# Tokens handed over transposed, norm scales applied behind the input projection, first keys taken as tokens land

## The chip, the cores and the metric

One core of a Trainium2 chip. The metric is the device time of one execution in microseconds (us). The engines are named as in the profile: PE (TensorE: matmuls and transposes; PEld its weight loads), DVE (VectorE), ACT (ScalarE), POOL (GpSimd), SP (SyncE, which issues nearly all DMAs of this kernel, in order).

## The reference

One block of a streaming encoder over 2048 tokens of 1024 channels, all in float32:

```python
h = rms_norm(x, norm_mix_g)                 # x * rsqrt(mean(x^2) + eps) * g
z = h @ w_in                                # 1024 -> 2568 columns
u_a, v_a = gelu(z[:512]), gelu(z[512:1024]) # gating heads
q, k, v  = z[1024:1536], z[1536:2048], z[2048:2560]
f        = z[2560:2568] + f_bias            # forget logits, one for each of 8 heads
out_a = u_a * (w_s @ layer_norm(v_a) + b_s) # in blocks of 128 tokens, w_s masked
out_b = softmax(q k^T / 8 + c[t] - c[s]) v  # s <= t, c = cumsum(log sigmoid(f))
x = x + concat(out_a, out_b) @ w_out
x = x + conv_ffn(rms_norm(x, norm_ffn_g))   # up, causal conv of width 3, gate, down
return rms_norm(x, norm_final_g)
```

## The kernel before

Matmuls run in single-pass float32 (`F32R`). To keep precision, both operands are split into a high and a low part, and `mm3` issues three matmuls for each 128 of the contraction: high x high, high x low, low x high. The split of a weight unit (128 x 1024 values, 512 KB) is `load_unit`: a DMA into `raw`, a cast to `whi` on POOL (`cast`), a difference `wlo` on DVE. There are two `raw` and five `whi`/`wlo` buffers.

Tokens are worked on in two halves of 1024, each of two chunks `b` of 512 (`TB`). Phase A (`phase_a`, `a_half`) computes the input projection. Half 0 goes: keys and queries, values, gating heads. Half 1 goes: gating heads, values, keys and queries. From the gating heads of half 0 on, the attention (`b_stream`) is interleaved with the projection: `tick` counts matmuls and takes a step of attention at a fixed rate; `defer` puts a piece of work a number of matmuls later. All later stages (output projection, feed-forward) follow with PE as the engine of most work.

The projection needs the tokens with channels on partitions, `hT[b]`, in high and low parts (`thi`, `tlo`). Before, `a_rows` loads rows of 128 tokens (tile `x`, four buffers), squares and sums them on ACT (L358), takes the power -1/2 on POOL (L362) and scales the rows on DVE (L366). `a_norm` transposes them on PE, four 128 x 128 transposes for each of eight channel groups of a chunk (L182), and splits the result out of PSUM with the norm's gain (ACT L191, DVE L192). For half 1 the rows are read twice: once for the scales alone and once, in column pieces that POOL scales (L399), for the transposes, which are deferred among the gating matmuls. The columns of gains, convolution weights and biases (`columns`, `columns_turn`) and the gating weights (`a_gate_w`) are transposed on PE too.

`channels` computes one key or query block: 128 channels x 512 tokens, 24 matmuls into a PSUM bank of tag `mm` (two buffers). ACT copies the high part out (L416), DVE takes the low part (L417), and four DMAs write both to DRAM (`kx`, `qx`) out of tile `vn` (four buffers). `a_forget` computes the forget logits of a chunk (16 matmuls against `wf`), and `cumulate` their running sum (matmuls against the triangle `tri`). PSUM has eight banks: two `mm`, two `tp`, three `s`, one `o`; the last four belong to attention.

The order on each engine's queue is set by the program order, `issue_after`, priorities, and the scheduler of the tile framework, which reorders instructions by a simulation of its own. An engine works its queue in order.

Of the kernel before, what the change touches and what calls it, by code (L numbers as in the profile page):

```python
# [32 lines left out]
AHEAD_B, AHEAD_W = 100, 2000  # L33
LAG = 2
# [17 lines left out]
def f32(ap):  # L52
    return ap.bitcast(F32)
# [26 lines left out]
class Block:  # L80
# [134 lines left out]
    def constants(self):  # L215
# [6 lines left out]
        self.colA = cp.tile([P, 112], F32, name="colA")  # L222
        self.colB = cp.tile([P, 88], F32, name="colB")
# [15 lines left out]
    def columns(self):  # L239

        nc, a = self.nc, self.a
        r0 = self.til(self.sp, [P, TB], F32, "st")[:112, :P]
        r1 = self.til(self.sp, [P, TB], F32, "st")[:88, :P]
        cv = a["w_conv"][0].rearrange("w (c p) -> w c p", p=P)
        self.dma(r0[0:8, :], a["norm_mix_g"][0].rearrange("(c p) -> c p", p=P))
        self.dma(r0[8:16, :], a["norm_ffn_g"][0].rearrange("(c p) -> c p", p=P))
        self.dma(r0[16:24, :], a["sg_b"][0])
        self.dma(r0[24:68, :], cv[0])
        self.dma(r0[68:112, :], cv[1])
        self.dma(r1[0:44, :], cv[2])  # L250
        self.dma(r1[44:88, :], a["b_conv"][0].rearrange("(c p) -> c p", p=P))
        self.rows_c = r0, r1
        self.g_mix = self.colA[:, 0:8]
        self.g_ffn = self.colA[:, 8:16]
        self.sgb = self.colA[:, 16:24]
        self.cw0 = self.colA[:, 24:68]
        self.cw1 = self.colA[:, 68:112]
        self.cw2 = self.colB[:, 0:44]
        self.cb = self.colB[:, 44:88]

    def columns_turn(self):
        nc = self.nc
        r0, r1 = self.rows_c
        for r, n, col in ((r0, 112, self.colA), (r1, 88, self.colB)):
            ps = self.til(self.ap, [P, TB], F32, "tp")
            nc.tensor.transpose(ps[:, :n], r, self.ident[:n, :n])
            nc.vector.tensor_copy(col, ps[:, :n])

        for t in (self.colA[:, 46:68], self.colA[:, 90:112], self.colB[:, 22:44], self.colB[:, 66:88]):
            nc.vector.tensor_scalar(t, t, 0.5, None, ALU.mult)  # L270


    def phase_a(self):
        tc = self.tc
        with ExitStack() as es:
# [4 lines left out]
            rows = self.a_rows(0, 0, True)  # L280
            self.columns()
            self.a_forget_w()
            self.a_norm(0, 0, rows, None, 0)
            self.first = []
            for c in range(2):
                with tc.issue_after(self.lo_ins[2 + 3 * c]):
                    self.first.append(self.a_unit("k", c))
            self.a_norm(0, 1, self.a_rows(0, 1, True), 16, 6)
            after = self.pow_ins

            def consts():
                with tc.issue_after(after):
                    self.a_consts(sp, pp)
                    self.b_consts()

            self.defer(16 + 6 * KC, consts)
# [9 lines left out]
    def a_forget_w(self):  # L306
        nc, a, kp = self.nc, self.a, self.sp
        wfr = kp.tile([P, 8, 8], F32, name="wfr")
        self.dma(wfr, self.w_in[:, :, 2560:2568])
        self.wf = kp.tile([P, 8, 16], F32R, name="wf")  # L310
        with self.tc.issue_after(self.rows_ins):
            nc.vector.tensor_copy(self.wf[:, :, 0:8], wfr)
            nc.vector.tensor_tensor(self.wf[:, :, 8:16], wfr, f32(self.wf[:, :, 0:8]), op=ALU.subtract)
        self.fb = kp.tile([P, 8], F32, name="fb")
        self.dma(self.fb, a["f_bias"].broadcast_to([P, 8]))
# [16 lines left out]
    def a_gate_w(self, sp, pp):  # L332

        nc, a = self.nc, self.a
        sw = self.til(sp, [P, 8, P], F32, "x")
        self.dma(sw, a["sg_w"][0].rearrange("h t s -> t h s"))
        nc.gpsimd.memset(sw[0:64, :, 64:128], 0.0)
        self.sw = sp.tile([P, 8, P], F32, name="sw")

        def turn(q):  # L340
            ps = self.transpose4(pp, "tp", [sw[:, 4 * q + i, :] for i in range(4)])
            nc.scalar.activation(self.sw[:, 4 * q:4 * q + 4, :].rearrange("p a b -> p (a b)"), ps, AF.Copy)

        self.defer(3, lambda: turn(0))
        self.defer(9, lambda: turn(1))

    def a_rows(self, half, b, keep):
# [5 lines left out]
        xs = []  # L353
        for i in range(4):
            x = self.til(sp, [P, D], F32, "x")
            self.dma(x, self.a["x"][0, t0 + i * P:t0 + (i + 1) * P, :])
            junk = self.til(sp, [P, D], BF16, "ln")
            nc.scalar.activation(junk, x, AF.Square, accum_out=ss[:, i:i + 1])  # L358
            xs.append(x)
        for q in [slice(i, i + 1) for i in range(4)] if keep else [slice(0, 4)]:  # L360
            nc.vector.tensor_scalar(rs[:, q], ss[:, q], 1.0 / D, EPS, ALU.mult, ALU.add)
            self.pow_ins = nc.gpsimd.tensor_tensor(rs[:, q], rs[:, q], self.mhalf[:, q], op=ALU.pow).ins  # L362
        if not keep:
            return rs
# [1114 lines left out]
```

## Time and profile before

| what | us |
|---|---|
| median of 3 runs (2466.55 to 2471.33) | 2469.13 |
| profiled execution, its own time | 2466.4 |
| span of the profiled execution | 2464.6 |
| PE busy in the span | 2420.7 |
| first projection matmul on PE starts | 13.87 |
| last query block of half 0 leaves PE at about | 125.6 |

Times inside an execution are counted from the start of the span. A row of the timeline gives start, duration, engine, line, operation, output<-inputs, and in brackets how long the engine was idle before it and what ended that. A row of the waits gives the total in us, the times, the longest.

### The profile page before, as it was taken

What the parts mean: (1) busy time and instruction counts of PE and PEld (TensorE: products, weight loads), DVE (VectorE), ACT (ScalarE), POOL (GpSimd) and SP (SyncE); (2) the same over time, 40 slices, a digit from 0 to 9 for tenths busy, and PEclk for the clock granted to TensorE, in tenths of its full rate; (3) what the DMA queues carried; (4) which work ended last, traced back from release to release, by engine and by line L of the source; (5) the groups of instructions that cost most, each with busy time, mean ns of one, the idle gap of its engine ahead of it and who ended that gap; (6) DMA issues with size and microseconds to landing.
All of it is one profiled execution on the core that took longest, in us unless ns stands there. A gap on an engine that the chain in (4) does not pass through costs nothing.

```text
span 2464.6 us, 32929 instructions
## 1 busy us (share of the span) xinstructions
PE 2420.7 (98%) x11082; PEld 1989.8 (81%) x11082; DVE 1740.5 (71%) x3060; ACT 1341.4 (54%) x2629; POOL 332.0 (13%) x335
## 2 busy tenths in 40 slices
PE   7999999999999999999999999999999999999998
PEld 5788878878878778788888878878888887888887
DVE  6237677565556777878878775488888887957775
ACT  4226676554355555767677673365555555444443
POOL 3214222010113311112111011100000000001000
PEclk9999999999999999999999999999999999999999
DMA  7863544767856544555555445412222329538633
GB/s 209 243 163 105 175 119 135 187 185 208 274 178 205 182 148 157 170 161 181 163 163 181 154 153 205 158 54 93 77 77 88 92 70 319 166 100 289 210 115 121
DMA packets 346244, 396.33 MB, mean 161 GB/s; under 512 B 52924, under 2 KB 222084, under 8 KB 344652
## 3 DMA queue, kind: packets, MB, share of 16 engines
q1 hardware_dynamic: 341036, 370.11, 48.8%
q0 software_dynamic: 5040, 24.12, 2.5%
q8 instruction: 88, 1.44, 0.3%
q14 instruction: 80, 0.66, 0.1%
HBM read 300.56 MB, written 93.72 MB: 160 GB/s over the span
## 4 chain that ended last, share of the span: by engine, by line
PE 88%; DMA 4%; DVE 3%; ACT 2%; issue 1%; POOL 1%; SPq 0%; POOLq 0%; DVEq 0%; ACTq 0%
PE D L1335 16%; PE mm L211 13%; PE mm L209 13%; PE mm L207 13%; PE A L1132 3%; PE A L1134 3%; PE A L1133 3%; PE o L774 2%; PE o L773 2%; PE s L786 2%; PE s L785 2%; PE s L725 2%; PE s L724 2%; PE B L1133 2%; PE B L1134 2%; PE B L1132 2%
## 5 line engine op out<-in xcount | busy, mean ns | idle before, releaser
L207 PE MATMUL mm<-thi,whi 128*128 128x512 f32 x960 | 377.4, 393 | 2.6 <-DVE vn L417 2.0
L209 PE MATMUL mm<-tlo,whi 128*128 128x512 f32 x960 | 377.5, 393 | 0.0
L211 PE MATMUL mm<-thi,wlo 128*128 128x512 f32 x960 | 376.4, 392 | 0.1
L207 PE MATMUL mm<-whi,thi 128*128 128x512 f32 x640 | 253.2, 396 | 1.1 <-DMA thi<-mixh 1.0
L211 PE MATMUL mm<-whi,tlo 128*128 128x512 f32 x640 | 251.1, 394 | 0.8 <-DMA tlo<-mixl 0.8
L209 PE MATMUL mm<-wlo,thi 128*128 128x512 f32 x640 | 250.8, 392 | 0.2 <-DVE wlo L161 0.2
L149 POOL TENSOR_SCALAR whi<-raw 128x1024 fp32r<-128x1024 f32 x108 | 126.5, 1172 | 908.4 <-PE mm L209 551.6
L733 ACT ACTIVATE s<-s,part 128x512 f32<-128x512 f32 (+3 forms) x257 | 150.8, 587 | 151.2 <-DVE part L728 85.4
L207 PEld LDWEIGHTS mm<-thi,whi 128*128 128x128 f32 x960 | 180.4, 188 | 41.8 <-DVE vn L417 2.3
L211 PEld LDWEIGHTS mm<-thi,wlo 128*128 128x128 f32 x960 | 180.5, 188 | 37.9 <-DVE wlo L161 0.6
L209 PEld LDWEIGHTS mm<-tlo,whi 128*128 128x128 f32 x960 | 180.5, 188 | 37.3
L797 DVE TENSOR_TENSOR pl<-e,ph 128x512 fp32r<-128x512 f32 (+2 forms) x212 | 136.7, 652 | 64.1 <-ACT ph L796 31.8
L161 DVE TENSOR_TENSOR wlo<-raw,whi 128x1024 fp32r<-128x1024 f32 x108 | 143.7, 1331 | 50.0 <-POOL whi L149 44.3
L791 ACT ACTIVATE e<-s 128x512 f32<-128x512 f32 (+2 forms) x227 | 116.1, 529 | 83.3 <-DVE s L789 41.6
L1335 PE MATMUL D<-wl,xh 128*128 128x512 f32 x368 | 141.5, 389 | 0.0
L1335 PE MATMUL D<-wh,xh 128*128 128x512 f32 x368 | 140.8, 389 | 0.2 <-DVE xo L1413 0.2
L207 PEld LDWEIGHTS mm<-whi,thi 128*128 128x128 f32 x640 | 120.6, 188 | 24.9 <-DMA thi<-mixh 1.4
L211 PEld LDWEIGHTS mm<-whi,tlo 128*128 128x128 f32 x640 | 120.3, 188 | 24.9 <-DMA tlo<-mixl 1.3
L209 PEld LDWEIGHTS mm<-wlo,thi 128*128 128x128 f32 x640 | 120.6, 188 | 23.2 <-DVE wlo L161 0.4
L1335 PE MATMUL D<-wh,xl 128*128 128x512 f32 x368 | 137.3, 389 | 0.0
L796 ACT ACTIVATE ph<-e 128x512 fp32r<-128x512 f32 (+2 forms) x212 | 117.2, 563 | 36.4 <-PE o L773 29.1
L728 DVE TENSOR_REDUCE part<-s 128x1 f32<-128x512 f32 x144 | 94.8, 683 | 28.3 <-PE s L725 27.6
(1885 smaller groups left out, 5786.3 us busy)
## 6 DMA issues: line engine op xcount, KB each, us to landing
raw<-in_w_up_dram SPq DMA_DIRECT2D x72, 512.0 KB
m<-kx SPq DMA_DIRECT2D x133, 256.0 KB
m<-kx SPq DMA_DIRECT2D x160, 136.0 KB
x<-act SPq DMA_DIRECT2D x84, 256.0 KB
raw<-in_w_in_dram SPq DMA_DIRECT2D x40, 512.0 KB
v<-vd SPq DMA_DIRECT2D x66, 256.0 KB
x<-in_x_dram SPq DMA_DIRECT2D x24, 512.0 KB
raw<-in_w_out_dram SPq DMA_DIRECT2D x24, 512.0 KB
```

The costliest lines, as they stand in the source:

```text
L149: self.cast_ins = self.nc.gpsimd.tensor_scalar(out, in_, 1.0, 0.0, ALU.mult, ALU.add).ins
L161: nc.vector.tensor_tensor(lo, raw, f32(hi), op=ALU.subtract)
L207: mm(ps, lhsT=ah[k], rhs=bh[k], start=k == 0, stop=False)
L209: mm(ps, lhsT=ah[k], rhs=bl[k], start=False, stop=False)
L211: self.last_mm = mm(ps, lhsT=al[k], rhs=bh[k], start=False, stop=k == n - 1).ins
L733: nc.scalar.activation(ps[:, :n], ps[:, :n], AF.Exp, scale=-1.0, bias=dst, accum_out=ls[:, tt, sb:sb + 1])
L796: nc.scalar.activation(ph[:, c], e[:, c], AF.Copy)
L797: nc.vector.tensor_tensor(pl[:, c], e[:, c], f32(ph[:, c]), op=ALU.subtract)
L1132: mm(ps, lhsT=xh[:, ks], rhs=yh[:, k, :], start=fresh and k == 0, stop=False, **kw)
L1133: mm(ps, lhsT=xh[:, ks], rhs=yl[:, k, :], start=False, stop=False, **kw)
L1134: mm(ps, lhsT=xl[:, ks], rhs=yh[:, k, :], start=False, stop=k == 3, **kw)
L1335: nc.tensor.matmul(bank[t], lhsT=x[i][:, ts], rhs=w[k], start=fresh and j == 0 and i + k == 0, stop=last and i == 1, **kw)
```

## The change

The host hands over four arrays laid out differently: the tokens transposed (`xT`, 1024 x 2048), the gating weights transposed (`sgT`), the forget columns of `w_in` as one row for each partition (`wf`), and all gains, convolution weights and biases as columns (`cols`). The transposes of these on PE go.

The scale 1/rms of a token commutes with the projection. So `hT` now holds the tokens times the gain alone (`a_split`, from SBUF, no transpose), and the scale is applied to what the projection gives. Where tokens lie on partitions (values, gating heads) it is the scale operand of the copy; forget logits take one more small DVE operation. Where tokens lie along the free dimension (keys, queries), `a_scales` spreads the scales over 128 partitions: an ACT copy of the four scale columns to 128 x 512, four transposes on PE, an ACT copy to `rb`. `channels` then has one more DVE operation: product with `rb` into a tile `st`, and the split into high and low from there.

The scales still need the rows: `a_rows` now loads them for the scales alone, in half 0 too (2 x 2 MB in addition there).

`a_start` replaces the beginning. It issues 24 transposes of the identity into an unused bank, then loads chunk 0 in eight tiles of 128 channels, with the first two key units in quarters between them, then two more key units (into `vn` buffers), the forget columns, chunk 1, and only then the rows for the scales. `first_keys` runs the first two key units of chunk 0 channel group by channel group, then units 3 and 4, the forget product, and the first two units of chunk 1: six blocks that stay in the six banks `mm`, `s` and `o` until the scales are there. Then come `a_scales` and the evacuations.

```diff
+WARM = 24
...
+    def a_start(self):
...
+            raw = v(raws[u])[:, ks, :]
+            self.dma(raw, self.w_in[:, ks, c0:c0 + P])
+            hi, lo = [t[:, ks, :] for t in parts[u]]
+            self.cast(hi, raw)
+            nc.vector.tensor_tensor(lo, raw, f32(hi), op=ALU.subtract)
...
+        for i in range(WARM):
+            nc.tensor.transpose(junk[:, i % 4 * P:(i % 4 + 1) * P], self.ident, self.ident)
+        self.hT[0] = self.parts(0)
+        xs = [self.til(sp, [P, 2, TB], F32, "x") for _ in range(4)]
+        for k in range(KC):
+            if k % 2 == 0:
+                unit(0, slice(k, k + 2))
+            self.dma(xs[k // 2][:, k % 2, :], self.a["xT"][k * P:(k + 1) * P, 0:TB])
+            self.a_split(0, k, xs[k // 2][:, k % 2, :])
+            if k % 2 == 0:
+                unit(1, slice(k, k + 2))
+        for u in (2, 3):
+            unit(u, slice(0, KC))
...
+        self.a_tokens(0, 1, None, 0)
+        self.scales[0] = [self.a_rows(0, b) for b in range(2)]
...
+    def a_scales(self, half, b):
...
+        w = self.til(sp, [P, 4, P], F32, "st")
+        nc.scalar.activation(w, self.scales[half][b].unsqueeze(2).broadcast_to([P, 4, P]), AF.Copy)
+        ps = self.transpose4(self.ap, "tp", [w[:, i, :] for i in range(4)])
+        nc.scalar.activation(self.rb[:, b, :], ps, AF.Copy)
+
+    def a_split(self, b, k, x):
+
+        hi, lo = self.hT[b]
+        self.nc.scalar.activation(hi[:, k, :], x, AF.Copy, scale=self.g_mix[:, k:k + 1])
+        self.nc.vector.scalar_tensor_tensor(lo[:, k, :], x, self.g_mix[:, k:k + 1], f32(hi[:, k, :]),
+                                            op0=ALU.mult, op1=ALU.subtract)
...
-            nc.scalar.activation(hi, ps, AF.Copy, scale=sc)
-            nc.vector.scalar_tensor_tensor(lo, ps, sc, f32(hi), op0=ALU.mult, op1=ALU.subtract)
+            t = self.til(sp, [P, TB], F32, "st")
+            nc.vector.scalar_tensor_tensor(t, ps, -0.125 if kind == "q" else 1.0, self.rb[:, b, :], op0=ALU.mult, op1=ALU.mult)
+            self.split_sb(t, hi, lo)
...
+        def first_keys():
+
+            banks = [self.til(pp, [P, TB], F32, "mm") for _ in range(2)] + [self.scores([P, TB]) for _ in range(3)]
+            banks.append(self.til(self.bpp, [P, TB], F32, "o"))
...
+            for k in range(KC):
+                for u in (0, 1):
+                    mms(u, 0, k)
+            for u, b in ((2, 0), (3, 0)):
+                for k in range(KC):
+                    mms(u, b, k)
+            self.a_forget(half, 0)
+            for u in range(2):
+                for k in range(KC):
+                    mms(u, 1, k)
+                self.a_scales(0, u)
+                for c in (range(2), range(2, 4))[u]:
+                    channels("k", c, None, None, 0, banks[c])
+            for u in range(2):
+                channels("k", u, None, None, 1, banks[u + 4])
+            for u in (2, 3):
+                channels("k", u, *self.first[u], 1)
+            self.a_forget(half, 1)
```

In the two listings of each place below, a row is line, operation, output<-inputs with the names of the program and a tile's number, shape, and how often. On PE's queue the program began with transposes of token rows, from tile `x`:

```order
L182 MATMUL mm_236<-ident,x_188 128x128
L182 MATMUL mm_241<-ident,x_188 128x128
L182 MATMUL s_246<-ident,x_188 128x128
L182 MATMUL s_251<-ident,x_188 128x128
L182 MATMUL s_256<-ident,x_188 128x128
L182 MATMUL o_261<-ident,x_188 128x128
```

Now it begins with the transposes of the identity and goes on with the first two units (`whi_190`, `whi_192`) in turn:

```order
L289 MATMUL tp_198<-ident 128x128 x24
L425 MATMUL mm_405<-thi_223,whi_190 128x512
L425 MATMUL mm_406<-thi_223,whi_192 128x512
L426 MATMUL mm_405<-tlo_225,whi_190 128x512
L427 MATMUL mm_405<-thi_223,wlo_191 128x512
L426 MATMUL mm_406<-tlo_225,whi_192 128x512
```

The transposes of tokens are gone there; key matmuls stand first. Further down on PE's queue, at the end of the first key block of before (`mm_374`), the transposes of chunk 1 (`x_316`, `x_320`) stood ahead of the second block:

```order
L211 MATMUL mm_374<-thi_233,wlo_304 128x512
L182 MATMUL tp_365<-ident,x_316 128x128
L182 MATMUL tp_381<-ident,x_316 128x128
L182 MATMUL tp_365<-ident,x_320 128x128
L182 MATMUL tp_381<-ident,x_320 128x128
L207 MATMUL mm_463<-thi_232,whi_309 128x512
```

Now, at the end of the sixth block (`o_410`), the small transposes of the forget logits and both sets of scale transposes (`st_581`, `st_631`) stand ahead of the seventh:

```order
L427 MATMUL o_410<-thi_293,wlo_193 128x512
L598 MATMUL tp_538<-ident,ln_524 128x16 x4
L183 MATMUL tp_583<-ident,st_581 128x128 x4
L183 MATMUL tp_633<-ident,st_631 128x128 x4
L208 MATMUL mm_675<-thi_292,whi_194 128x512
```

PE thus meets the scales after 160 matmuls and meets both at once. On SP's queue, the two key units followed the rows and constants of chunk 0, and the rows of chunk 1 came next:

```order
L99 DMA raw_302<-in_w_in_dram 128x8x128
L99 DMA raw_308<-in_w_in_dram 128x8x128
L99 DMA lng<-in_sg_ln_g_dram 128x512
L99 DMA x_316<-in_x_dram 128x1024
L99 DMA x_320<-in_x_dram 128x1024
```

Now, behind chunk 0 and four key units, chunk 1 (`in_xT_dram`) and three query units (`raw_784`, `raw_790`, `raw_984`) stand ahead of or among the rows for the scales:

```order
L100 DMA raw_784<-in_w_in_dram 128x8x128
L100 DMA x_314<-in_xT_dram 128x2x512
L100 DMA raw_790<-in_w_in_dram 128x8x128
L100 DMA x_322<-in_x_dram 128x1024
L100 DMA x_326<-in_x_dram 128x1024
L100 DMA x_330<-in_x_dram 128x1024
L100 DMA raw_984<-in_w_in_dram 128x8x128
L100 DMA x_334<-in_x_dram 128x1024
L100 DMA x_342<-in_x_dram 128x1024
L100 DMA x_346<-in_x_dram 128x1024
L100 DMA x_350<-in_x_dram 128x1024
L100 DMA x_354<-in_x_dram 128x1024
```

The row tiles moved behind all of the first half's tokens and seven weight units.

226 lines of the change are left out of this document (98 added, 128 removed).

## The prediction

> **What bounds the kernel now.** I read the page first, then the start by windows of 25 us, the waits of PE (TensorE), and the timeline up to 130 us.
>
> ```profile
> span 2464.6 us, 32929 instructions
> PE 2420.7 (98%) x11082; PEld 1989.8 (81%) x11082; DVE 1740.5 (71%) x3060; ACT 1341.4 (54%) x2629; POOL 332.0 (13%) x335
> ```
>
> PE is busy for 98% of the span, so a microsecond counts only if PE stops waiting for it or stops spending it. The windows (us, then busy time and count of PE, PEld, DVE, ACT, POOL, granted clock, DMA share, GB/s) show where PE is not full:
>
> ```profile
> 0.00:25.00 25.00, 15.59 (x75) 10.69 (x76) 13.27 (x32) 16.07 (x27) 7.96 (x18) 1.00 0.84 266
> 25.00:50.00 25.00, 21.58 (x114) 15.25 (x115) 17.93 (x31) 8.54 (x15) 13.28 (x22) 1.00 0.50 135
> 75.00:100.00 25.00, 23.04 (x104) 18.59 (x103) 6.95 (x10) 8.40 (x16) 11.65 (x17) 1.00 0.89 289
> ```
>
> Of the 43.9 us that PE idles in the whole span, 12.8 lie in the first 50. The waits of PE up to 120 us name them:
>
> ```profile
> PE mm L182 <- DVE rstd L361: 7.5, 1, 7.5
> PE tp L182 <- DVE tlo L192: 2.3, 2, 1.5
> PE mm L207 <- DVE vn L417: 2.0, 1, 2.0
> ```
>
> First PE waits for the first row scale, then for the splits of the second chunk, and once for a bank that a key block has not left. The timeline gives the milestones:
>
> ```profile
> 1.19 0.29 POOL masks.py:199 TENSOR_SCALAR_AFFINE_SELECT ident<-ident 128x128 f32<-128x128 f32 x1
> 4.61 1.06 ACT L358 ACTIVATE ln<-x 128x1024 bf16<-128x1024 f32 x1 [2.54 <-DMA x<-in_x_dram]
> 13.87 0.40 PE L566 MATMUL mm<-thi,wf 128*16 128x512 f32 x1 [0.80 <-DVE tlo L192]
> 48.49 0.41 PE L603 MATMUL tp<-tri,fr 128*8 128x512 f32 x1
> 49.65 0.44 PE L207 MATMUL mm<-thi,whi 128*128 128x512 f32 x1
> ...
> 49.94 0.39 PE L209 MATMUL mm<-tlo,whi 128*128 128x512 f32 x1
> ...
> 59.04 0.39 PE L211 MATMUL mm<-thi,wlo 128*128 128x512 f32 x1
> ...
> 125.66 0.60 ACT L416 ACTIVATE vn<-mm 128x512 fp32r<-128x512 f32 x1 [4.99 <-PE mm L211]
> ```
>
> No matmul of the projection starts before 13.87. From 49.94 to 59.04 lie 40 matmuls at one after another: 9.10 / 40 = 0.2275 us each. The key and query blocks of half 0 hold 16 x 24 = 384 such matmuls, the two forget products 32: 416 x 0.2275 = 94.6 us. The last block leaves PE at about 125.6 (the evacuation that waited for PE starts at 125.66). So 31 us of these 125.6 are not projection. By 49.65 PE has done three blocks and both forget products (104 matmuls, 23.7 us): 26 of the 31 lie ahead of that point.
>
> **The change, part by part.** *Transposes of tokens.* Price of four in a stream of matmuls:
>
> ```profile
> 42.72 0.60 PE L182 MATMUL tp<-ident,x 128*128 128x128 f32 x4
> 43.08 0.48 PE L568 MATMUL mm<-tlo,wf 128*16 128x512 f32 x1
> 43.40 0.39 PE L209 MATMUL mm<-tlo,whi 128*128 128x512 f32 x1
> ```
>
> From 42.72 to 43.40 stand four transposes and one matmul: 0.68 - 0.23 = 0.45 us for four. In half 1 the 16 groups of four go (7.2 us, all in a stretch where PE is nearly full), and two groups for the scales come (0.9): -6.3. Those of half 0 are counted in the milestones below, as are the 8 of the gating weights.
>
> *The start.* The 24 transposes of the identity can begin once it stands (1.19 + 0.29). Their price is that of the first and of the later transposes of before:
>
> ```profile
> 7.97 0.85 PE L182 MATMUL s<-ident,x 128*128 128x128 f32 x3
> 8.62 0.42 PE L182 MATMUL o<-ident,x 128*128 128x128 f32 x1
> ...
> 10.84 0.49 PE L182 MATMUL s<-ident,x 128*128 128x128 f32 x3
> ...
> 11.17 0.27 PE L182 MATMUL o<-ident,x 128*128 128x128 f32 x1
> ```
>
> Three take 0.65 us (0.22 each) at 8 us, and 0.33 (0.11 each) some 3 us after the first one. So 24 take about 13 x 0.22 + 11 x 0.11 = 4.1 us: until about 5.7. What the first matmul needs lands at about the same time. DMA paces:
>
> ```profile
> 7.43 1.06 ACT L358 ACTIVATE ln<-x 128x1024 bf16<-128x1024 f32 x1 [0.42 <-DMA x<-in_x_dram]
> 8.86 1.06 ACT L358 ACTIVATE ln<-x 128x1024 bf16<-128x1024 f32 x1 [0.27 <-DMA x<-in_x_dram]
> 14.71 1.04 POOL L149 TENSOR_SCALAR whi<-raw 128x1024 fp32r<-128x1024 f32 x1 [3.62 <-DMA raw<-in_w_in_dram]
> 16.45 1.47 POOL L149 TENSOR_SCALAR whi<-raw 128x1024 fp32r<-128x1024 f32 x1 [0.71 <-DMA raw<-in_w_in_dram]
> ```
>
> Consecutive tiles of 512 KB land 1.43 us apart for tokens and 1.74 for weight units; the first tile was there at 4.61, so about 3.2 us pass before the first data. Columns, the first quarter of a unit and the first token tile are about 0.5 MB: 3.2 + 1.4 = 4.6, and the first split on ACT 0.6: 5.3. I take the first matmul at 5.8. Chunk 0 with two units is 2 x 1.74 + 4 x 1.43 = 9.2 us of DMA, landed at 12.4, while PE needs 48 x 0.2275 = 10.9 us from 5.8: PE is the slower of the two. Units 3 and 4 land at 14.2 and 15.9; cast and difference take 1.17 and 1.22 (rows below), so they are ready when PE gets there at 16.7. Chunk 1 is not needed before 5.8 + (96 + 16) x 0.2275 = 31.3. PE runs 160 matmuls through, to 5.8 + 36.4 = 42.2.
>
> ```profile
> L358 ACT ACTIVATE ln<-x 128x1024 bf16<-128x1024 f32 x16 | 16.9, 1055 | 15.2 <-DMA x<-in_x_dram 14.9
> L161 DVE TENSOR_TENSOR wlo<-raw,whi 128x1024 fp32r<-128x1024 f32 x13 | 15.8, 1218 | 3.8 <-POOL whi L149 3.7
> L149 POOL TENSOR_SCALAR whi<-raw 128x1024 fp32r<-128x1024 f32 x13 | 15.2, 1169 | 31.6 <-PE mm L209 21.7 <-DMA raw<-in_w_in_dram 5.2 <-issue 4.6
> L417 DVE SCALAR_TENSOR_TENSOR vn<-mm,vn 128x512 fp32r<-128x512 f32 x16 | 11.0, 689 | 32.8 <-ACT vn L416 26.7 <-DMA qx<-vn 4.9 <-DMA kx<-vn 1.2
> L362 POOL TENSOR_TENSOR rstd<-rstd,mhalf 128x1 f32<-128x1 f32 (+1 forms) x10 | 7.2, 721 | 35.0 <-DVE rstd L361 35.0
> ```
>
> *The new wait.* All six banks are then full, and PE's next work stands behind the transposes of both scales; the second needs all eight row tiles of half 0, 4 MiB that before did not read separately. Ahead of and with them SP issues 7 weight units (12.2 us), 8 tiles' worth of transposed tokens and 8 of rows (16 x 1.43 = 22.9), columns and layer-norm gains (1.0): 36.1 us, last landing at 39.3. Square 1.06, a small DVE step, power 0.72: about 41.3. That beats PE's 42.2 by a hair. The chain behind (two sets of transposes with ACT copies of 0.6 between, DVE 0.69 to free the first bank) still costs PE 2 to 3 us, nothing covers it, and the third unit's block of chunk 1 starts at about 45.0. The power waits in POOL's queue behind the cast of a query unit, which waits for the first unit's last use (about 36.7 + 1.2): early enough.
>
> *The rest of half 0.* 256 matmuls (58.2), two cumulations at 49.65 - 48.49 = 1.16, small transposes 0.4: 45.0 + 60.9 = 105.9. SP must write six blocks at once:
>
> ```profile
> 77.78 2.37 SPq L99 DMA_DIRECT2D kx<-vn  x4
> ```
>
> 2.4 us each, 14 us, and the constants besides. A bank is now free after one DVE operation that needs no ACT, so PE has some 11 us of cover; if the write buffers hold DVE longer, the query blocks are late next. I allow one wait like the 2.0 at L417: 107.9, against 125.6 before: -17.7.
>
> *Added evacuation.* 32 x 0.69 = 22 us of DVE. Half 0 has room (6.95 of 25 above). In half 1 it is 11 us beside this:
>
> ```profile
> 525.00:550.00 25.00, 25.00 (x119) 20.04 (x118) 15.90 (x42) 15.97 (x33) 2.11 (x2) 1.00 0.47 123
> ```
>
> PE is full while DVE works 64%; about 2 us more in each 25 stays under 75%. Nought to 4 us; I take 0. Scaled copies of values and gates keep their count. POOL loses 32 scalings that PE does not wait for: 0.
>
> **Sum**: -17.7 - 6.3 = -24.0. The profiled execution took 2466.4 (span 2464.6 and 1.8 around it), so 2442.4; it stands 2.7 under the median of 2469.13, so a median of 2445.1.
>
> **Rivals.**
>
> *Scales come later.* Over windows of 10 us the DMA rate varied:
>
> ```profile
> 10.00:20.00 10.00, 8.53 (x47) 5.79 (x46) 8.40 (x19) 5.85 (x11) 3.06 (x3) 1.00 0.95 284
> 20.00:30.00 10.00, 9.40 (x44) 6.58 (x43) 7.41 (x13) 4.57 (x9) 7.37 (x13) 1.00 0.68 194
> ```
>
> The queue up to the last row tile is 12.4 MB. At 284 GB/s throughout it lands at 46.9, and by the same steps the blocks resume at about 51: 6 later, 2451. For it: token tiles wait for four buffers. Against: 1.43 us per 512 KB is 367 GB/s. Chance 0.16.
>
> *Slower: the same wait, long.* At the second window's 194 GB/s the last tile lands at 67 and PE resumes at 71.5, 26 later: 2471. Break-even is at 200 GB/s; at 175 it is 2478. For it: one SP queue issues everything in order, and a unit waiting for its buffer stops the row tiles behind it. Against: the 194 was an emptied queue (DMA share 0.68), and the units ahead of the last row tile wait for buffers that are freed before 30 us. Chance 0.03.
>
> *Given back later.* Attention is interleaved with half 1, and the order of both changes far past this stage. PE there waits for others already:
>
> ```profile
> 225.00:250.00 25.00, 23.11 (x122) 19.56 (x122) 23.28 (x38) 14.87 (x25) 15.54 (x9) 1.00 0.56 164
> PE s L724 <- DMA m<-kx: 2.5, 1, 2.5
> PE o L774 <- DVE pl L797: 2.1, 2, 1.7
> PE s L758 <- DVE m L742: 1.9, 1, 1.9
> ```
>
> About 31 us of idle lie behind 50 us; if they grew by three quarters, the gain would be gone: 2468. For it: DVE at 93% there. Against: the change adds nothing to DVE there. Chance 0.06. If the three waits shown, all before 400 us (6.5 us), vanish instead, since PE's transposes and their banks are gone: 2439, chance 0.10.
>
> *No warm start.* Should transposes not raise the clock, the first 3 us of matmuls would go at half pace, 1.5 us later: 2447, chance 0.05. The rows speak against it: pace doubled during transposes alone. The Trainium skill, "TensorE: Matmul & The Clock Gate", Part 4, says that the full clock "doesn't engage" for transposes, as they don't count as PE activity; the trace disagrees (0.22 to 0.11 us).
>
> **Numbers.** The forecast, 2445, has the remaining 0.60. The range of 2433 to 2457 takes in the late scales (2451) with 4 us of DVE wait and the measurement on one side, and the vanished waits with no new stall at the scales (2439 - 6) on the other. A measurement of this kernel tells 0.2% (4.9 us) from no change. Faster: 0.60 + 0.16 + 0.10 + 0.05 = 0.91; the same: 0.06; slower: 0.03.
>
> **What would show it.** Right: the first projection matmul near 6 us; no PE wait over 1 us until about 42, then 2 to 3 us for the second scale's transposes; the last query block's evacuation near 108; PE's instruction count 98 lower; DVE busy time some 20 us higher. Wrong: matmuls of the first two units waiting on token tiles beyond 17 us, the resumption behind 50, or more PE waits between 225 and 400 us than the 6.5 shown.

## The result and the profile after

The changed kernel takes 2444.85 us (median of 2441.62 to 2448.11), the kernel before on the same chip 2467.84 (2464.51 to 2471.33): a ratio of 0.9907, interval 0.9887 to 0.9927. The forecast was 2445.0. The total came out; one of its two terms did not.

The page of the changed kernel, profiled in an execution of 2441.62 us:

```profile
span 2439.9 us, 32802 instructions
PE 2410.8 (99%) x10984; PEld 1982.3 (81%) x10984; DVE 1750.5 (72%) x3086; ACT 1350.3 (55%) x2635; POOL 315.9 (13%) x303
```

PE's busy time falls by 9.9 us and its idle time by 14.8 (43.9 to 29.1). The first two windows of 25 us (columns as in the prediction) are where most of the idle time went:

```profile
0.00:25.00 25.00, 21.96 (x100) 18.19 (x101) 16.48 (x30) 10.97 (x15) 7.22 (x18) 1.00 0.94 279
25.00:50.00 25.00, 23.68 (x110) 17.76 (x109) 9.20 (x19) 16.10 (x29) 9.89 (x16) 1.00 0.93 327
```

PE works 45.64 of these 50 us, against 37.17 before, and the DMA share stands at 0.94 and 0.93 where it was 0.84 and 0.50. PE's waits of more than 1 us from its first matmul or transpose up to 120 us (total, times, longest):

```profile
PE tp L183 <- ACT st L358: 1.3, 1, 1.3
PE mm L425 <- ACT thi L365: 1.3, 1, 1.3
```

The 7.5 us for the first row scale is gone, and nothing waits for token tiles. Two waits are left that matter: one for the first split (L365) and one for the second scale's copy (L358). The timeline shows both, and the last query block of half 0:

```profile
1.54 4.38 PE L289 MATMUL tp<-ident 128*128 128x128 f32 x24 [1.54 <-POOL ident masks.py:199]
5.04 1.28 ACT L365 ACT_TABLE_LOAD   x1 [5.04 <-DMA x<-in_xT_dram]
6.33 2.20 ACT L365 ACTIVATE thi<-x,cols 128x512 fp32r<-128x512 f32 x3
7.20 0.70 PE L425 MATMUL mm<-thi,whi 128*128 128x512 f32 x2 [1.27 <-ACT thi L365]
...
41.68 1.06 ACT L347 ACTIVATE ln<-x 128x1024 bf16<-128x1024 f32 x1
43.11 1.02 POOL L349 TENSOR_TENSOR rstd<-rstd,mhalf 128x4 f32<-128x4 f32 x1 [2.93 <-DVE rstd L348]
44.83 0.66 PE L183 MATMUL tp<-ident,st 128*128 128x128 f32 x4
45.52 0.60 ACT L360 ACTIVATE u<-tp 128x512 f32<-128x512 f32 x1 [1.55 <-PE tp L183]
46.13 0.62 ACT L358 ACTIVATE st<-rstd 128x512 f32<-128x512 f32 x1
46.80 0.66 PE L183 MATMUL tp<-ident,st 128*128 128x128 f32 x4 [1.32 <-ACT st L358]
47.22 0.48 PE L208 MATMUL mm<-thi,whi 128*128 128x512 f32 x1
...
109.70 0.69 DVE L398 SCALAR_TENSOR_TENSOR st<-mm,u 128x512 f32<-128x512 f32 x1 [1.42 <-PE mm L212]
```

The first tile is there at 5.04, but ACT then loads its function table for 1.28 us before it splits it: the first matmul starts at 7.20. (In the kernel before this load ran from 0.79, ahead of the first data.) The last query block's evacuation begins at 109.70, against 125.66 before: 16.0 us earlier.

Where the rest of the 24.7 us of span went is read from four marks: that evacuation, the first tanh of the feed-forward (ACT, 771.8 before and 753.7 after), the first matmul of the second half's up projection (1612.4 and 1585.5), and the end. Windows cut near these marks, of the kernel before and then of the changed one, columns as above:

```profile
126.00:772.00 646.00, 636.15 (x3076) 525.33 (x3075) 396.55 (x796) 351.84 (x723) 135.29 (x114) 1.00 0.61 177
772.00:1612.00 840.00, 831.61 (x3781) 684.05 (x3780) 619.01 (x1194) 513.60 (x1110) 144.75 (x139) 1.00 0.52 166
```

```profile
110.00:754.00 644.00, 636.29 (x3034) 523.37 (x3033) 405.20 (x826) 364.85 (x737) 129.30 (x98) 0.99 0.62 184
754.00:1586.00 832.00, 828.34 (x3777) 683.40 (x3775) 615.37 (x1184) 508.91 (x1101) 143.98 (x139) 1.00 0.52 167
```

By the marks: 16.0 us from the start, 2.2 from there to the tanh (attention and half 1, where 64 transposes left PE), 8.8 from the tanh to the up projection, and 2.2 lost at the end. Sum: 16.0 + 2.2 + 8.8 - 2.2 = 24.8, which is the 24.7 but for rounding.

The change touches no instruction behind the tanh, but the tanh does not cut the same work in both kernels, since attention is interleaved. PE's busy time and count on attention's tile `t` between the tanh and the up projection, before and then after:

```profile
771.82:1612.42 840.60, 221.80 (x797) 1.00 0.52 166
753.69:1585.52 831.83, 217.64 (x786) 1.00 0.52 167
```

On tile `v` it has 306 matmuls for 312, on the tiles `mm` 2450 for 2443: ten fewer in all, and 10 x 0.2275 = 2.3 us of the 8.8 are work that the changed kernel has done ahead of the mark. The two stages together hold the same work but for the transposes; they are worth 11.0 us (1486.8 to 1475.8), of which 6.9 are less idle time of PE (18.3 to 11.4). Between the evacuation and the tanh idle time also moved: PE stands 0.4 us instead of 7.2 between 225 and 425, but 6.6 instead of 0.8 between 575 and 700. These two windows of the changed kernel hold most of the latter:

```profile
670.00:680.00 10.00, 6.77 (x24) 4.11 (x24) 8.63 (x15) 8.38 (x20) 0.00 (x0) 0.86 0.39 129
680.00:690.00 10.00, 8.80 (x25) 6.19 (x26) 4.69 (x16) 6.12 (x17) 0.00 (x0) 0.63 0.57 184
```

Some 24 matmuls each stand where a full window holds about 47: 4.4 us idle, and a granted clock of 0.86 and 0.63, so that the matmuls which do run take longer. Busy time hides that loss.

### The profile page after: what moved, and what is told of

It reads as the page before. It is cut to its first block, busy times and chain, and to the rows that moved or that the text cites. A ratio compares the mean times of both kernels' runs of the same rounds, so it can differ in the third digit from the quotient of the medians.

```text
span 2439.9 us, 32802 instructions
## 1 busy us (share of the span) xinstructions
PE 2410.8 (99%) x10984; PEld 1982.3 (81%) x10984; DVE 1750.5 (72%) x3086; ACT 1350.3 (55%) x2635; POOL 315.9 (13%) x303
## 4 chain that ended last, share of the span: by engine, by line
PE 84%; DMA 6%; DVE 5%; issue 2%; ACT 1%; SPq 1%; POOL 1%; DVEq 0%; POOLq 0%; ACTq 0%
PE mm L208 13%; PE mm L210 13%; PE mm L212 13%; PE D L1358 10%; PE A L1155 3%; PE A L1157 3%; PE A L1156 3%; PE o L797 2%; PE o L796 2%; PE s L747 2%; PE s L748 2%; PE s L809 2%; PE s L808 2%; PE B L1156 2%; PE B L1157 2%
## 5 line engine op out<-in xcount | busy, mean ns | idle before, releaser
L208 PE MATMUL mm<-thi,whi 128*128 128x512 f32 x912 | 358.0, 393 | 0.6 <-DVE st L398 0.6
L210 PE MATMUL mm<-tlo,whi 128*128 128x512 f32 x912 | 358.2, 393 | 0.0
L212 PE MATMUL mm<-thi,wlo 128*128 128x512 f32 x912 | 357.8, 392 | 0.0
L150 POOL TENSOR_SCALAR whi<-raw 128x1024 fp32r<-128x1024 f32 (+1 forms) x112 | 125.9, 1125 | 1014.5 <-PE mm L210 567.1
L208 PEld LDWEIGHTS mm<-thi,whi 128*128 128x128 f32 x912 | 171.5, 188 | 36.4 <-DVE st L398 1.1
L210 PEld LDWEIGHTS mm<-tlo,whi 128*128 128x128 f32 x912 | 171.4, 188 | 35.1
L212 PEld LDWEIGHTS mm<-thi,wlo 128*128 128x128 f32 x912 | 171.5, 188 | 34.8
L162 DVE TENSOR_TENSOR wlo<-raw,whi 128x1024 fp32r<-128x1024 f32 x104 | 133.7, 1285 | 59.4 <-POOL whi L150 58.8
L814 ACT ACTIVATE e<-s 128x512 f32<-128x512 f32 (+2 forms) x216 | 110.6, 529 | 82.5 <-DVE s L812 39.8
```

The lines of the kernel that those rows point to most:

```text
L150: self.cast_ins = self.nc.gpsimd.tensor_scalar(out, in_, 1.0, 0.0, ALU.mult, ALU.add).ins
L162: nc.vector.tensor_tensor(lo, raw, f32(hi), op=ALU.subtract)
L208: mm(ps, lhsT=ah[k], rhs=bh[k], start=k == 0, stop=False)
L210: mm(ps, lhsT=ah[k], rhs=bl[k], start=False, stop=False)
L212: self.last_mm = mm(ps, lhsT=al[k], rhs=bh[k], start=False, stop=k == n - 1).ins
L814: nc.scalar.activation(e[:, c], ps[:, c], AF.Exp, scale=-1.0)
```

## The experiments

Medians in us, each with the kernel before measured beside it; marks from one profiled execution each. Two profiled executions of code that is the same can differ: the last stage alone, from the up projection's mark to the end, took between 851.3 and 855.3 us in the kernels below, though none of them changes it. Differences of up to 4 us between marks so far apart are therefore not read. The start of the kernel before isn't one number either: up to the first mark, PE has the same 518 instructions in the same order in the kernel before, e6 and e10, and the mark stands at 125.66, 128.90 and 127.72. Much of that is matmuls at half pace behind waits (last section). So the start's 16.0 us could as well have read 18 or 19. The changed start, which waits less, repeats better: 109.29 to 109.78 in the changed kernel, e1, e2 and e5.

| kernel | median | ratio to before, interval | last query evacuation | to tanh | tanh to up |
|---|---|---|---|---|---|
| before | 2467.84 | 1 | 125.66 | 646.2 | 840.6 |
| changed | 2444.85 | 0.9907 [0.9887, 0.9927] | 109.70 | 644.0 | 831.8 |
| e1 half 1 on PE | 2443.14 | 0.9906 [0.9891, 0.9920] | 109.29 | 644.5 | 833.1 |
| e2 rate 3.6 | 2445.75 | 0.9915 [0.9900, 0.9931] | 109.78 | 646.4 | 834.8 |
| e3 table early | 2443.13 | 0.9909 [0.9894, 0.9924] | 108.61 | 644.7 | 834.0 |
| e4 no transposes ahead, one execution | 2445.74 | | 112.23 | 646.7 | 831.9 |
| e5 POOL back | 2442.81 | 0.9897 [0.9882, 0.9911] | 109.43 | 645.1 | 834.8 |
| e6 before, no POOL | 2470.23 | 1.0009 [0.9999, 1.0019] | 128.90 | 642.7 | 841.1 |
| e7 start from rows | 2459.82 | 0.9966 [0.9953, 0.9979] | 121.57 | 646.3 | 837.2 |
| e8 later spread | 2441.49 | 0.9891 [0.9874, 0.9908] | 107.79 | 643.1 | 835.8 |
| e9 half 1 only | 2482.53 | 1.0060 [1.0046, 1.0074] | 130.41 | 661.1 | 837.9 |
| e10 before, lag 36 | 2469.03 | 1.0000 [0.9989, 1.0011] | 127.72 | 648.7 | 840.1 |
| e11 e8, lag 36 | 2449.89 | 0.9929 [0.9916, 0.9942] | 107.96 | 645.9 | 841.1 |
| e12 e8, lag 24 | 2443.32 | 0.9911 [0.9895, 0.9928] | 108.11 | 645.9 | 834.3 |

### e1: half 1's transposes back on PE

```diff
 def a_tokens(self, half, b, wait, gap):
+    if half:   # rows in column pieces, transposed by PE as before, unscaled
+        ...
+        self.defer(wait + c * gap, lambda: self.transpose_split(...))
+        return
```

> The changed kernel, but the tokens of half 1 are read as rows again and transposed on PE (64 transposes in 16 groups, without the scaling of rows; the scales stay behind the projection). Theory: of the 24 us, about 16 come from the start and the rest from half 1: 16 groups x 0.45 us = 7.2 us come back, and the PE waits between 225 and 425 us (7.2 us of idle before, 0.4 after) come back in part, so 6 to 12 us slower than the changed kernel: 2451 to 2457, about 0.994 of before. Milestone: the last query block of half 0 still leaves PE at 109 to 111 us. Rival: the start is all of the gain; then within 2 us of the changed kernel.

Measured: 2443.14, no slower than the changed kernel (2444.85). The page and the window of the old waits:

```profile
PE 2415.3 (99%) x11048; PEld 1988.6 (82%) x11048; DVE 1756.0 (72%) x3086; ACT 1349.4 (55%) x2635; POOL 312.8 (13%) x303
225.00:425.00 200.00, 199.36 (x1049) 168.20 (x1048) 147.14 (x295) 144.36 (x269) 43.76 (x27) 1.00 0.52 155
```

The 64 transposes are there again (11048 instructions instead of 10984) and cost PE 4.5 us of busy time, but the idle time is 22.9 us instead of 29.1. The waits between 225 and 425 stay away (0.6 us) though PE transposes there. Between the last query evacuation and the up projection e1 gains 9.2 us over the kernel before, with these transposes in place (the changed kernel gains 11.0). So neither the forecast's price for these transposes nor its reading that the waits hung on them holds.

### e2: attention at a faster rate

```diff
-RATES = [3.5, 4.0, 4.4, 3.6]
+RATES = [3.5, 3.6, 4.4, 3.6]
```

> The changed kernel with attention taken in steps of 3.6 instead of 4.0 matmuls in half 1. Theory: in the changed kernel the projection of half 1 ends 40 us earlier than before while attention does not, so attention is left over at 575 to 700 us without matmuls to hide its latency: 6.6 us of PE idle there against 0.8 before, and a granted clock of 0.90 from 650 to 700. With more attention inside half 1 the idle from 575 to 700 falls under 3 us and the time by 3 to 6 us, to about 2440. Rival: the waits only move (to 225 to 450 us, where DVE is at 82 to 88%), and the time stays within 2 us of the changed kernel.

Measured: 2445.75, and PE idles 6.5 us between 575 and 700 (6.6 in the changed kernel). The hole at 670 to 690 isn't a matter of this rate.

### e3: the function table loaded ahead

```diff
+        early = cp.tile([P, 8], F32, name="early")
+        nc.scalar.activation(early, self.mhalf, AF.Copy)
```

> The changed kernel with one small ACT copy (128 x 8) added ahead of everything, so that ACT's table load does not stand between the first token tile and its split. Theory: the first projection matmul starts at 5.9 instead of 7.2 us, PE keeps that lead until the scales, and the seventh key block starts 0.7 to 1.3 us earlier than 47.2; the whole gains about 1 us, less than the times can show. Rival: the token tiles pace PE (one in 1.2 us), so the first matmul is earlier but waits appear between 6 and 18 us and the first two blocks end at the same time; the seventh block starts at 47.2.

Measured: 2443.13. The load, PE's first instructions and the copy's wait in its timeline:

```profile
0.80 1.28 ACT L224 ACT_TABLE_LOAD   x1 [0.80 <-PEq L1503]
1.53 5.32 PE L291 MATMUL tp<-ident 128*128 128x128 f32 x24 [1.53 <-POOL ident masks.py:199]
6.57 0.93 PE L427 MATMUL mm<-thi,whi 128*128 128x512 f32 x2
...
45.75 0.66 PE L183 MATMUL tp<-ident,st 128*128 128x128 f32 x4 [1.32 <-ACT st L360]
46.16 0.48 PE L208 MATMUL mm<-thi,whi 128*128 128x512 f32 x1
```

The load now runs while the first data are on their way. PE starts 0.6 us earlier and not the expected 1.3, since it now waits for no data but finishes its 24 transposes first (5.32 us here, 4.38 in the changed kernel). The seventh block starts 1.06 us earlier (46.16 for 47.22) with the copy's wait unchanged at 1.32; the last evacuation follows by 1.09. That wait is made by the order on ACT and not by the landing of the rows: in the changed kernel the second scale is there at 44.13 (43.11 + 1.02), but ACT begins its copy at 46.13, behind the copy of the first spread at 45.52, which waited for PE's first transposes. In the whole time 1 us cannot be told.

The Trainium skill, "ScalarE: Activation LUTs", section "What ACT_TABLE_LOAD costs", gives about 1283 ns for the load and about 1380 ns of drain with every switch to a different set. The 1.28 agrees. The drain does not show: in the changed kernel the split starts at 6.33, directly behind the load's end at 5.04 + 1.28. ACT had nothing to drain there, but in the middle of its work, in the kernel before, a load at 336.41 also follows directly on an activation (335.33 + 1.06), and the next one starts at 337.71.

### e4: no transposes ahead of the first matmul

```diff
-WARM = 24
+WARM = 0
```

> The changed kernel without the 24 transposes of the identity at the start. Theory: transposes do raise PE's pace (in the kernel before they went from 0.22 to 0.11 us each within 3 us), so without them the first matmuls, from about 7.2 us on, stand 0.43 to 0.46 us apart for some 3 us and the first two blocks end about 1.5 us later. Rival (the Trainium skill, TensorE: Matmul & The Clock Gate, Part 4, by which transposes do not count as activity): the transposes change nothing, the first matmuls stand 0.23 us apart or equally slow with and without them.

Measured in one execution: 2445.74. PE's first matmuls, whose pace is the distance of their starts:

```profile
7.82 1.19 PE L425 MATMUL mm<-thi,whi 128*128 128x512 f32 x2 [7.82 <-ACT thi L365]
8.81 0.63 PE L426 MATMUL mm<-tlo,whi 128*128 128x512 f32 x1
9.23 0.63 PE L427 MATMUL mm<-thi,wlo 128*128 128x512 f32 x1
...
13.07 0.70 PE L425 MATMUL mm<-thi,whi 128*128 128x512 f32 x2
13.61 0.40 PE L426 MATMUL mm<-tlo,whi 128*128 128x512 f32 x1
13.84 0.40 PE L427 MATMUL mm<-thi,wlo 128*128 128x512 f32 x1
```

They start 0.43 us apart until 13.07 and 0.23 apart behind it: 5.2 us at half pace, though the granted clock reads 1.00 over this stretch. In the changed kernel the pace is 0.23 from 8.46 on. The last evacuation begins at 112.23, 2.5 us later. Of these, 0.6 have nothing to do with the transposes: the first token tile landed later (5.66 for 5.04) and the first matmul started at 7.82 for 7.20. The other 1.9 are the pace: the first twelve matmuls take 5.25 us here and 3.34 in the changed kernel. So the transposes do bring PE to full pace, and they are worth about 1.9 us at the start (1.5 was the rival's price). The Trainium skill, "TensorE: Matmul & The Clock Gate", Part 4, says that transposes don't; the runs disagree (0.43 us without them, 0.23 with them).

### e5 and e6: POOL's row scalings

Of e5 the lines beside e1's, of e6 the whole edit:

```diff
+                for i in range(4):     # e5: in half 1 of e1
+                    nc.gpsimd.tensor_scalar(x[:, i, :], x[:, i, :], self.ones1[:, i:i + 1], 0.0, ALU.mult, ALU.add)
...
-            for i in range(4):         # e6: in half 1 of the kernel before
-                nc.gpsimd.tensor_scalar(x[:, i, :], x[:, i, :], rows[:, i:i + 1], 0.0, ALU.mult, ALU.add)
```

> The kernel is that of e1 (half 1's tokens transposed on PE from rows), and POOL multiplies the 32 row pieces of half 1 by 1.0, as the kernel before did with the row scales; the norm scales stay behind the projection. Theory: what half 1 gained over the kernel before is the 32 POOL scalings that stood between a token row's landing and its transposes; with them back the idle time of PE between 225 and 425 us, 0.6 us in e1, returns to 5 to 8 us, and the time is 4 to 8 us above e1's 2443.1: 2447 to 2451. Rival: the scalings cost nothing and the gain there comes from how the order behind the start falls; then PE idles under 2 us in that stretch and the time is 2441 to 2445.

> The kernel before without POOL's 32 scalings of half 1's token rows; half 1's tokens go unscaled into the projection, everything else as before. Theory: the scalings held PE between 225 and 425 us (7.2 us idle there before); without them that falls under 2 us and the time is 2460 to 2463, 5 to 8 us under the kernel before. Rival: they cost nothing, the waits stay or move, and the time is within 2 us of the kernel before, 2466 to 2470.

Measured: 2442.81 and 2470.23. The stretch of the old waits, in e5 and then in e6:

```profile
225.00:425.00 200.00, 200.00 (x1059) 169.64 (x1058) 145.98 (x296) 145.85 (x269) 52.14 (x43) 1.00 0.54 156
```

```profile
225.00:425.00 200.00, 192.81 (x1010) 162.37 (x1009) 150.76 (x298) 137.09 (x259) 53.45 (x30) 1.00 0.49 144
```

With the scalings back PE never stands there; without them in the kernel before it stands 7.2 us as ever. The theory is refuted from both sides; POOL's work there cost nothing, as forecast.

### e7: the start from rows

```diff
-            self.dma(xs[k // 2][:, k % 2, :], self.a["xT"][k * P:(k + 1) * P, 0:TB])
-            self.a_split(0, k, xs[k // 2][:, k % 2, :])
...
+        rows = load(0)     # row tiles, for the scales and for the transposes below
+        for c in range(KC):
+            got.append(self.transpose4(*at[c], [x[:, c * P:(c + 1) * P] for x in rows]))
...
-                first_keys()
+                self.a_forget(half, 0)
+                self.a_scales(0, 0)
+                channels("k", 0, *u0, 0)
+                ...
```

> The changed kernel with half 0 started from rows: one set of row tiles serves both the scales and the transposes of PE (32 transposes ahead of the first block, 32 deferred between blocks for the second chunk), whole weight units, no keys staged as columns land, 4 MiB less to load; the norm scales are still applied behind the projection. Theory: the transposed load and the staging in eighths by columns give the larger part of the start's 16 us, since PE has 416 matmuls to do and otherwise cannot begin until a whole set of rows has landed; then the last query block's evacuation begins at 116 to 119 us (109.7 in the changed kernel, 125.7 before), and the time is 2451 to 2455. Rival: most of the 16 us was the row scale standing ahead of the transposes (PE's 7.5 us wait for it and what followed); then the evacuation begins at 109 to 112 and the time is 2444 to 2447.

Measured: 2459.82. PE's waits up to 130 us, longest first:

```profile
PE mm L183 <- DMA x<-in_x_dram: 5.3, 1, 5.3
PE mm L208 <- POOL whi L150: 3.4, 2, 1.9
```

The last query evacuation begins at 121.57, 11.9 us behind the changed kernel's. So the larger part of the 16.0 us at the start comes with the transposed load and the staging, as the theory had it, though its 116 to 119 was missed. The other 4.1 (125.66 to 121.57) come with what e7 keeps of the change: the scales behind the projection, and the gating weights and columns that need no transposes. They are hardly more than what the mark of the kernel before moves by itself (up to 3.2). PE begins at 5.25 with transposes of tokens, which are not among the 416 matmuls; the first of those comes at 13.06, two waits for whole weight units (1.5 and 1.9) stand at 13.06 and 15.73, and from there to 21.00 matmuls run at half pace. The time is above what was expected (2451 to 2455): the span is 18.1 us over the changed kernel's, of which the start explains 11.9; 2.3 come up to the tanh and 5.4 in the stage behind it, with 1.5 less at the end.

### e8: the second scale's spread behind the next block's first products

```diff
-                self.a_scales(0, u)
+                if u == 0:
+                    self.a_scales(0, 0)
...
+            self.defer(15, lambda: self.a_scales(0, 1))
+            channels("k", 2, *self.first[2], 1)
```

It has e3's early load as well.

> The table load early as in e3, and the spread of the second row scale deferred behind the first products of the next key block, so that PE does not stand at the copy between two sets of transposes. Theory: the next key block no longer waits for the second scale; its first matmul comes 0.3 to 0.5 us earlier than e3's 46.16, the last query block's evacuation begins at 108.1 to 108.4 (108.61 in e3), and the time is within 1 us of e3's 2443.1. Rival: the block then waits for a free bank instead, since every bank holds products that cannot be evacuated before their scale; then nothing moves, or up to 2 us are lost (2445).

Measured: 2441.49. The seventh block:

```profile
45.79 0.50 PE L208 MATMUL mm<-thi,whi 128*128 128x512 f32 x1 [1.41 <-DVE st L400]
```

The block starts 0.37 us earlier than in e3; its wait is now for a bank (1.41 for DVE's evacuation), as the rival had it, but shorter than what it replaces (1.32 for the copy and 0.41 of transposes behind it). The last evacuation begins at 107.79. Its median is the lowest of all, 3.4 us under the changed kernel's, though the intervals overlap.

### e9: half 1 alone

```diff
-            self.scales[0][b] = rs          # beside e7: half 0 scaled ahead of PE
+            for i, x in enumerate(xs):
+                nc.vector.tensor_scalar(x, x, rs[:, i:i + 1], None, ALU.mult)
...
+            if half == 0:
+                nc.scalar.activation(hi, ps, AF.Copy, scale=sc)
+                nc.vector.scalar_tensor_tensor(lo, ps, sc, f32(hi), op0=ALU.mult, op1=ALU.subtract)
```

> Half 1 as in the changed kernel (tokens handed over transposed, scales applied behind the projection), half 0 as before: rows scaled before PE transposes them, scales nowhere applied later in half 0, whole weight units. Theory: the 7 us that PE idled between 225 and 425 us before vanish through what half 1 no longer does; then PE idles under 2 us there, the last query block's evacuation begins at 124 to 127 us as before, and the time is 2459 to 2463. Rival: those waits vanish only with the new start; then 5 us or more of them stay, or return elsewhere before 800 us, and the time is 2464 to 2469.

Measured: 2482.53, slower than the kernel before by 0.6%, which neither theory expected. PE's largest waits up to 130 us, and its window from 225 us:

```profile
PE mm L208 <- DVE vn L412: 9.8, 3, 5.8
```

```profile
225.00:425.00 200.00, 193.12 (x966) 161.50 (x965) 144.36 (x280) 138.01 (x242) 56.09 (x33) 0.99 0.46 139
```

PE again stands 6.9 us there, now mostly for ACT. The start is 4.8 us later than before (three waits of together 9.8 for evacuations, where the kernel before has one of 2.0), and 14.9 are lost from there to the tanh. So what half 1 no longer does brings no gain by itself. Why this start is the slowest of all was not tested.

### e10 to e12: one number of a deferral

```diff
-GATE_LAG = 30
+GATE_LAG = 36
```

e10 is this edit in the kernel before, e11 in e8; e12 has 24 in e8.

> The kernel before with one number changed: the transposes and writes of a gating block are deferred by 36 matmuls instead of 30. It moves work and takes none away. Theory: the waits between 225 and 425 us are a matter of what stands ahead of what in the queues (the key load of the 2.5 us wait at 345 us stood in SP's queue behind a write that waited for such a transpose); then the idle time in that stretch moves by over 3 us from its 7.2, and the time by 2 to 6 us either way. Rival: they are a shortage of an engine there; then the idle time stays at 6 to 8 us and the time at 2466 to 2469.

> The kernel of e8 with the same number 36 instead of 30. By the theory of e10 its idle time behind 425 us (14 us in e8 from 425 to 1000) moves by several us without a reason in the work; the time is 2437 to 2447. By the rival nothing moves and it is within 1 us of e8's 2441.5.

> The kernel of e8 with the deferral of the gating transposes at 24 matmuls (30 in e8: 2441.5; 36 in e11: 2449.9). Theory of queue order: the start up to the values is as in e8 (108.5 us), and behind it the time falls anywhere between 2437 and 2450, in idle time of PE behind 425 us. Rival: a smooth effect of the lag, by which 24 gives about 8 us less than 30: 2432 to 2436.

Measured: 2469.03, 2449.89 and 2443.32. In the kernel before the idle time between 225 and 425 fell from 7.2 to 4.9, by 2.3 where the theory asked for over 3, and the time didn't move: by its own numbers e10 speaks against the theory, and the rival's 6 to 8 us of idle time did not stay either. In e8 the same edit costs 8.4 us, with intervals that do not touch, and 24 costs nothing that can be told, so the effect isn't smooth. Its start is the same (107.96); these are the stages from the tanh to the up projection, e8 and then e11:

```profile
751.00:1587.00 836.00, 833.10 (x3798) 687.46 (x3797) 624.81 (x1190) 514.00 (x1107) 147.38 (x143) 1.00 0.52 168
```

```profile
754.00:1595.00 841.00, 832.02 (x3780) 686.60 (x3778) 612.93 (x1183) 510.48 (x1102) 143.32 (x139) 1.00 0.51 166
```

e11 takes 5 us more there with 6.1 us more of idle time, in a stage long after the gating blocks; it even has fewer matmuls there (786 for 792 on tile `t`, 306 for 312 on `v`). In e11 PE's waits between these two marks read, largest first:

```profile
PE s L812 <- DMA m<-kx: 2.8, 2, 2.1
PE dn L751 <- DMA t<-cc: 2.5, 2, 2.3
PE s L813 <- DMA m<-kx: 1.8, 1, 1.8
```

All three are attention's loads, which SP issues in order; in e8 no load is among the waits of this stage. Shown is that the order alone can move 8 us behind the start. The 8.8 us which the changed kernel gains in that stage may be such a case. It isn't shown: the kernels with the new start have 832 to 836 there, e11 alone 841, and those with the old one 840 to 841 (e7 and e9, which start from rows with half 1 as in the changed kernel, 837 and 838). The moved work does not explain it away, since e1 and e5, which have 794, 312 and 2443 matmuls on the three tiles where the kernel before has 797, 312 and 2443, are 7.5 and 5.8 us shorter there. Why this start mostly comes with the better order stays open.

## Why the prediction was right, and where it was not

**The start, -17.7: measured -16.0.** The mechanism was as told: no wait on token tiles, PE running on to the scales, one chain there. The term that was mis-sized is the first matmul. It was put at 5.8, from 1.4 for DMA and 0.6 for the split; the table load of 1.28 was not counted, and it came at 7.20. The 160 matmuls then took 0.8 longer than put, nearly all of it among the first four, which start 0.31, 0.62 and 0.34 apart. The scales' chain was sized rightly: 2.8 us were put for it (42.2 to 45.0), and from the end of the 160 (the last starts at 44.16, so 44.39) to the seventh block at 47.22 are 2.8. So the block came 2.2 late, 1.4 by the first matmul and 0.8 by the matmuls behind it. The last landing at 39.3 and the power by 41.3 were early: ACT's last square began at 41.68, back to back with those ahead of it, and the power ended at 44.13. That cost PE nothing, since ACT did not come to the second copy before 46.13. Behind that, 60.9 and an allowed wait of 2.0 stand against 62.5 (47.22 to 109.70).

**Half 1's transposes, -6.3: no such gain.** This is the step that failed. The work is worth 4.5 us of PE's busy time (e1), not 7.2, and taking it away moved no time that can be measured: e1 and e5, which have it, are no slower. That they lie "all in a stretch where PE is nearly full" was read from busy shares; the kernels have holes of waiting too, and with the transposes back there is less idle time (22.9 us in e1 for 29.1 in the changed kernel).

**The rival of the vanished waits.** The 6.5 us between 225 and 400 did vanish, in every kernel with the new start, with PE's transposes or without, with POOL's scalings or without (and in e7). The time did not go to 2439: 5.8 us of new idle time came between 575 and 700, and the 6.3 of the transposes, which that figure takes in, did not come. Its reason, "PE's transposes and their banks are gone", does not hold: in e1 PE transposes there through the same banks, and the waits stay away.

**Costed at nothing: DVE and POOL.** DVE rose by 10.0 us, not by 20: its row scalings (6.9 us for eight) left with the change and were not subtracted. PE did not notice. POOL's scalings cost nothing (e5, e6).

**No warm start.** The rows of the trace held (e4); the price is about 1.9 us where 1.5 was put.

**What was missed** is a gain behind the start that is not the transposes': of the 11.0 us between the last evacuation and the up projection e1 has 9.2 with the transposes in place. By the marks 8.8 of it, or 6.5 without the attention that was done earlier, lie in a stage that the change does not touch. It more than stands in for the failed 6.3, and a start 1.7 short and 2.2 lost at the end take the rest back, so the total came out. That is luck: a total that fits is no proof of its terms.

## What to carry to other kernels

At the start of a kernel, count what the first matmul needs, and let PE begin on the first eighth of it; anything that commutes with the work (here the norm scale) belongs behind it. Look for the first function-table load: a tiny activation ahead of the first data hides it (1.1 us here, e3). Where work is interleaved, check that a mark cuts the same work in both kernels before the stages are compared. And where a scheduler sets the order, let a gain or loss of a few microseconds far from the edit be tested with an unrelated shift of the order before it is explained.

## What the runs showed of the hardware beyond that

A wait of PE can cost more than its length. Behind the 2.5 us wait of the kernel before, its timeline has:

```profile
344.96 0.65 PE L724 MATMUL s<-m,t 96*128 96x512 f32 x1 [2.51 <-DMA m<-kx]
...
346.69 0.63 PE L207 MATMUL mm<-whi,thi 128*128 128x512 f32 x1
347.12 0.63 PE L209 MATMUL mm<-wlo,thi 128*128 128x512 f32 x1
```

Up to 348.40 matmuls start 0.43 us apart instead of 0.23: 3.4 us at half pace, about 1.6 us lost beside the wait itself, and counted as busy. The granted clock reads 0.66 from 345 to 350. Half pace does not follow every wait. Here is the same place in the same order of instructions, in the kernel before and then in e6:

```profile
86.34 0.50 PE L207 MATMUL mm<-thi,whi 128*128 128x512 f32 x1 [1.96 <-DVE vn L417]
...
89.88 0.39 PE L207 MATMUL mm<-thi,whi 128*128 128x512 f32 x1
90.10 0.39 PE L209 MATMUL mm<-tlo,whi 128*128 128x512 f32 x1
```

```profile
87.98 0.50 PE L207 MATMUL mm<-thi,whi 128*128 128x512 f32 x1 [1.79 <-DVE vn L415]
...
89.74 0.63 PE L207 MATMUL mm<-thi,whi 128*128 128x512 f32 x1
90.17 0.63 PE L209 MATMUL mm<-tlo,whi 128*128 128x512 f32 x1
```

The wait of 1.96 us leaves the pace at 0.23. Behind the shorter one of 1.79 it is 0.43 from 89.32 to 92.30, and the granted clock reads 0.66 from 88 to 93. So single executions of the same start differ by some us. Nor is the way to full pace the same each time: the same 24 transposes at the start took 4.38 us in the changed kernel, 4.41 in e12, 5.32 in e3 and 5.38 in e8.
